# A transformer layer in one core: the sample's gate/up stage started with eight PSUM banks and DVE-made operands, its out operand loaded earlier, GpSimd storing its own sums

## The chip, the core and the metric

The kernel runs on one core of a Trainium2 chip. The core has five engines that work side by side and meet through semaphores: TensorE (PE in the profile) does matmuls into eight PSUM banks; VectorE (DVE) and ScalarE (ACT) do elementwise work and are the two engines here that read PSUM; GpSimd (POOL) does elementwise work between SBUF tiles; SyncE (SP) issues DMAs. ACT and POOL issue DMAs too, each in the order of its own queue. The metric is the device time of one execution in microseconds (us), as a median over executions.

## The reference

One layer of a hybrid encoder, with the same weights for two batches: the prompt ("p", 512 tokens) and the sample ("s", 1024 tokens), width 1024, in float32.

```
h  = rmsnorm(x);  proj = h @ w_in                      # 1024 x 4096
o_hgrn = two-way gated recurrence, 4 heads of 128;  o_na = 2-D neighbourhood attention, 8 heads of 64
x  = x + concat(o_hgrn, o_na) @ w_out                  # 1024 x 1024
h2 = rmsnorm(x)
x  = x + (silu(h2 @ w_gate) * (h2 @ w_up)) @ w_down    # 1024 -> 2816 -> 1024
```

## The kernel before

Every large product keeps float32 accuracy by splitting each operand into a rounded high part (a cast on ACT) and the rest (a subtraction on DVE) and by adding three matmuls: high by high, high by low, low by high. So a tile that a product reads costs one ACT and one DVE instruction first (`split`, `load_w`).

The stages follow each other: input projection with recurrence and attention of the prompt, then of the sample; the prompt's out projection and its 22 gate/up units with the sample's attention woven in; the sample's out projection (`out_units("s", ...)`); its gate/up stage (`gate_s`); the down projection of both (`down_all`). Tile, the layer in which the kernel is written, puts the instructions of each engine in a fixed order by its own estimate of when each can run, and an earlier place in the program gives it precedence. So an engine's order is not the program's, but it can't change at run time. A pool of SBUF tiles that opens where another closed makes its first writers wait for the old tiles' last readers.

The parts that matter here:

- **Out operand of the sample.** `load_oT` reads the attention's result back in 16 pieces of 128x512, by DMAs in POOL's queue into two buffers, and splits each piece on ACT and DVE. The first 8 (tokens 0 to 511) are called for in `late`, four units before the end of the prompt's gate units; the other 8 in `later`, at the start of the out projection. The out projection takes 4 tiles of 128 tokens at a time, each with its own `pd` bank, and DVE's L945 adds the residual and frees the bank.
- **Gate/up of the sample** uses Strassen's scheme in Winograd's form: per pair of output blocks j (11 of them) and per weight w (0 gate, 1 up), seven products P1 to P7 of 12 matmuls each instead of eight. Their token-side operands are A11, A12, A22 and four sums S1 = A21+A22, S2 = S1-A11, S3 = A11-A21, S4 = A12-S2, where A11 to A22 are quarters of the normalized h2 (`araw`, f32). The weight side needs sums too (T2, T3 and two in place), 4 per w. `norm2` normalizes tile t of 128 tokens as the out projection finishes it and lets `gate_s` start at t = 5: A11, A12 (tokens 0 to 511) and the first weights. `run`, called in `tail` after all eight norms, makes A22 and S1 to S4: sums on POOL (L1135, L1137, L1143) and one on DVE (L1136), then splits, and only then goes through the products. P1+P2, P6+P7 and P5+P3 share a bank of each w. Weight sums of all j are POOL's (L1084, L1092), in one buffer `t` for T2 and T3.
- **Stores.** `store_g` makes four sums of each finished block on POOL and stores seven tiles to DRAM, all seven DMAs in ACT's queue (L1027).
- **Down** reads these back (`wst<-g_A`), loads its weights `B`, splits both on ACT and DVE (L1031, L1032), and runs 18 matmuls a step.

## Time and profile before

| | |
|---|---|
| median of 3 runs | 2022.0 us (2020.91 to 2022.23) |
| the profiled execution, its own time | 2023.84 us |
| its span, first to last instruction | 2021.7 us |
| TensorE matmuls busy | 1950.9 us, 96% of the span |
| VectorE, ScalarE, GpSimd busy | 1261.4, 808.1, 384.4 us |
| mean granted TensorE clock | 0.986 of full speed |

The profile holds one execution. A busy TensorE is not TensorE at full speed: the granted clock says whether it ran at 2.4 GHz (1.00) or at 1.2 GHz (0.50). An instruction's row gives its start, its duration, engine, source line, operation and tiles, and in brackets how long its engine had been idle before it and what ended that.

### The profile page before, as it was taken

What the parts mean: (1) busy time and instruction counts of PE and PEld (TensorE: products, weight loads), DVE (VectorE), ACT (ScalarE), POOL (GpSimd) and SP (SyncE); (2) the same over time, 40 slices, a digit from 0 to 9 for tenths busy, and PEclk for the clock granted to TensorE, in tenths of its full rate; (3) what the DMA queues carried; (4) which work ended last, traced back from release to release, by engine and by line L of the source; (5) the groups of instructions that cost most, each with busy time, mean ns of one, the idle gap of its engine ahead of it and who ended that gap; (6) DMA issues with size and microseconds to landing.
All of it is one profiled execution on the core that took longest, in us unless ns stands there. A gap on an engine that the chain in (4) does not pass through costs nothing.

```text
span 2021.7 us, 28466 instructions
## 1 busy us (share of the span) xinstructions
PE 1950.9 (96%) x10546; PEld 1577.8 (78%) x10546; DVE 1261.4 (62%) x2485; ACT 808.1 (40%) x1477; POOL 384.4 (19%) x326
## 2 busy tenths in 40 slices
PE   7999999999999999998999997899999998999998
PEld 5777887778787778777888776678888887888887
DVE  7677535475775757765755238766666664676643
ACT  5544345553443444654554115323233232433332
POOL 1200000000000010010102123454443441642400
PEclk9999999999999999998999999899999999999999
DMA  7832364433123156454555631132332324854443
GB/s 236 267 95 88 95 214 133 128 106 95 32 74 100 32 181 194 128 162 131 155 140 166 217 125 52 42 118 86 118 107 89 110 92 170 270 184 150 138 142 113
DMA packets 235297, 266.54 MB, mean 132 GB/s; under 512 B 19653, under 2 KB 168155, under 8 KB 234903
## 3 DMA queue, kind: packets, MB, share of 16 engines
q1 hardware_dynamic: 188448, 186.30, 30.9%
q10 hardware_dynamic: 41079, 61.27, 8.5%
q0 software_dynamic: 5632, 17.17, 2.6%
q8 instruction: 83, 1.36, 0.3%
q14 instruction: 55, 0.45, 0.1%
HBM read 194.84 MB, written 70.20 MB: 131 GB/s over the span
## 4 chain that ended last, share of the span: by engine, by line
PE 81%; DVE 5%; DMA 5%; issue 4%; ACT 3%; POOL 2%; ACTq 0%; POOLq 0%; DVEq 0%
PE pd L1037 19%; PE pm L1037 13%; PE pd L180 7%; PE pd L181 7%; PE pd L182 7%; PE pd L167 6%; PE pd L168 6%; PE pd L169 6%; PE pm L311 3%; PE pm L599 1%; PE pm L613 1%; PE pm L631 1%; PE pm L446 1%; DMA wst<-in_w_in_dram 1%; DVE w L110 1%
## 5 line engine op out<-in xcount | busy, mean ns | idle before, releaser
L110 DVE TENSOR_TENSOR w<-wst,w 128x1024 fp32r<-128x1024 f32 x128 | 158.6, 1239 | 120.6 <-ACT w L109 113.6
L109 ACT CAST w<-wst 128x1024 fp32r<-128x1024 f32 x128 | 134.2, 1050 | 184.2 <-PE pd L182 71.7
L1037 PE MATMUL pd<-bo,ao 128*128 128x512 f32 x792 | 194.9, 393 | 5.5 <-ACT bo L1031 5.5
L1037 PEld LDWEIGHTS pd<-bo,ao 128*128 128x128 f32 x792 | 150.2, 190 | 37.6 <-ACT bo L1031 5.9
L1037 PE MATMUL pm<-bo,ao 128*128 128x512 f32 x594 | 147.2, 390 | 0.0
L180 PE MATMUL pd<-h2p,w 128*128 128x512 f32 (+1 forms) x368 | 143.3, 389 | 0.6 <-ACT h2p L144 0.5
L181 PE MATMUL pd<-h2p,w 128*128 128x512 f32 (+1 forms) x368 | 141.6, 385 | 0.0
L182 PE MATMUL pd<-h2p,w 128*128 128x512 f32 (+1 forms) x368 | 141.4, 384 | 0.0
L1037 PE MATMUL pd<-opS,w 128*128 128x512 f32 x528 | 132.9, 401 | 7.8 <-DVE u L1154 3.0
L1037 PE MATMUL pm<-opS,w 128*128 128x512 f32 x528 | 129.2, 393 | 2.7 <-DVE opS L1032 1.4
L167 PE MATMUL pd<-w,hs 128*128 128x512 f32 x320 | 131.4, 411 | 0.0
L1037 PEld LDWEIGHTS pm<-bo,ao 128*128 128x128 f32 x594 | 111.8, 188 | 23.3
L1037 PE MATMUL pd<-opA,w 128*128 128x512 f32 x528 | 129.9, 394 | 0.0
L922 POOL DMA_DIRECT2D ost<-ot_p x8 | 4.3, 541 | 647.6 <-ACT Kn L373 632.4
L1037 PEld LDWEIGHTS pd<-opS,w 128*128 128x128 f32 x528 | 101.6, 194 | 32.7 <-DVE opS L1032 4.6
L169 PE MATMUL pd<-w,hs 128*128 128x512 f32 x320 | 126.4, 395 | 0.0
L168 PE MATMUL pd<-w,hs 128*128 128x512 f32 x320 | 126.2, 395 | 0.0
L1037 PEld LDWEIGHTS pm<-opS,w 128*128 128x128 f32 x528 | 99.6, 189 | 25.0 <-DVE opS L1032 2.6
L1037 PEld LDWEIGHTS pd<-opA,w 128*128 128x128 f32 x528 | 99.1, 189 | 24.1 <-ACT s L1181 3.8
L1031 ACT CAST w<-wst 128x512 fp32r<-128x512 f32 x110 | 65.0, 620 | 114.0 <-PE pd L1037 57.6
L1032 DVE TENSOR_TENSOR w<-wst,w 128x512 fp32r<-128x512 f32 x110 | 99.9, 923 | 16.4 <-ACT w L1031 16.0
L1032 DVE TENSOR_TENSOR bo<-B,bo 128x512 fp32r<-128x512 f32 x55 | 50.8, 924 | 76.7 <-ACT bo L1031 76.7
(233 smaller groups left out, 4314.2 us busy)
## 6 DMA issues: line engine op xcount, KB each, us to landing
wst<-in_w_in_dram SPq DMA_DIRECT2D x68, 512.0 KB, 4.1
wst<-in_w_gate_dram SPq DMA_DIRECT2D x44, 512.0 KB, 4.0
wst<-in_w_up_dram SPq DMA_DIRECT2D x44, 512.0 KB, 3.9
wst<-g_S SPq DMA_DIRECT2D x44, 384.0 KB, 3.2
wst<-g_A SPq DMA_DIRECT2D x33, 384.0 KB, 3.8
g_S<-S ACTq DMA_DIRECT2D x44, 256.0 KB, 2.0
pj_s<-ev ACTq DMA_DIRECT2D x40, 256.0 KB, 2.3
bias<-bias_d SPq DMA_DIRECT2D x192, 48.0 KB, 2.6
```

The source lines that it names most:

```text
L109: act.copy(out=w[:, 0, :], in_=s)
L110: dve.tensor_tensor(out=w[:, 1, :], in0=s, in1=f32(w[:, 0, :]), op=ALU.subtract)
L167: pe.matmul(ps, lhsT=xh, rhs=w[:, 0, j, :], start=k == 0, stop=False)
L168: pe.matmul(ps, lhsT=xh, rhs=w[:, 1, j, :], start=False, stop=False)
L169: pe.matmul(ps, lhsT=xl, rhs=w[:, 0, j, :], start=False, stop=k == NK - 1)
L180: pe.matmul(ps[:, ts], lhsT=wv[:, 0, k, :], rhs=xh, start=k == 0, stop=False)
L181: pe.matmul(ps[:, ts], lhsT=wv[:, 0, k, :], rhs=xl, start=False, stop=False)
L182: pe.matmul(ps[:, ts], lhsT=wv[:, 1, k, :], rhs=xh, start=False, stop=k == NK - 1)
L311: pe.matmul(ps[i * 64:i * 64 + 64, c * 64:c * 64 + 64], lhsT=lhsT[:, c * 128 + i * 64:c * 128 + i * 64 + 64], rhs=rhs(c * 128 + i * 64), s ...
L1031: act.copy(out=dst[0], in_=src)
L1032: dve.tensor_tensor(out=dst[1], in0=src, in1=f32(dst[0]), op=ALU.subtract)
L1037: pe.matmul(ps, lhsT=l[a], rhs=r[b_], start=start and i == 0, stop=stop and i == 2, skip_group_check=more)
```

## The change

1. Both halves of the sample's out operand are loaded in `late`, among the prompt's last gate units; the raw quarters of h2 (`araw`) take the place of the second half's pool in `later`.
2. For the first pair (j = 0) the products of both weights alternate: P1, P2, P4 and P5 of gate and up go to eight banks of their own (four `pd`, four `pm`) before any is read; P6, P7 and P3 follow. P1 starts when norm 5 is done; norms 6 and 7 are called for between products.
3. A22 and the sums for S1 to S4 are made on DVE, the first of them in two token parts (0 to 383 of the quarter, then the last 128) in instructions of 2x384, 4x128 or 2x512 columns. S1 and S2 go to the pool of the out operand's second half. The weight sums of j = 0 go to DVE as well; those of j = 1 to 10 stay on POOL.
4. In the later pairs s3 overwrites s1, and there are two buffers for s2.
5. `store_g` leaves the stores of A11 and A22 in ACT's queue and puts the other five (A12, S1 to S4) in POOL's, which made four of them. It serves the prompt's units and the sample's alike.

```
-    xs, h2, gate = {}, {}, {}
+    xs, h2, gate, araw = {}, {}, {}, {}
...
             else:
-                h2[b, u] = [pls["araw"].tile([128, 4, 512], F32, name=f"a{u}{g}")
-                            for g in range(2)]
+                if u == 0:
+                    for k in ((1, 1), (0, 0), (1, 0), (0, 1)):
+                        araw[k] = pls["araw"].tile([128, 4, 512], F32, name="a%d%d" % k)
+                h2[b, u] = [araw[u, g] for g in range(2)]
         sink = to_tiles(h2[b, u], t % 4) if b == "p" else \
...
         for k in ASIDE:
-            act.dma_start(out=g_d[k][j][:, c0:c0 + n], in_={**A, **S}[k])
+            (act if k in ("A11", "A22") else st).dma_start(out=g_d[k][j][:, c0:c0 + n],
+                                                           in_={**A, **S}[k])
...
-        def operand(name, src, where):
+        def place(name, where):
...
                 A[name] = [[t[:, 0, :], t[:, 1, :]] for t in o]
-            elif where == "actR1":
-                o = [pls[where].tile([128, 2, 4, 512], F32R, tag="actT", bufs=2, name=f"op{name}")]
-                A[name] = [[o[0][:, i, k, :] for i in range(2)] for k in range(4)]
             else:
-                o = pls[where].tile([128, 2, 4, 512], F32R, name=f"op{name}")
+                o = pls[where].tile([128, 2, 4, 512], F32R, name=f"op{name}",
+                                    **({} if where == "aop" else {"tag": "actT", "bufs": 2}))
                 A[name] = [[o[:, i, k, :] for i in range(2)] for k in range(4)]
-            for k in range(4):
-                split(A[name][k], src[:, k, :])
+                whole[name] = o
+        whole = {}
+        def fill(name, src, ts=slice(0, 512), step=1):
+            for k in range(0, 4, step):
+                if step == 1:
+                    split([h[:, ts] for h in A[name][k]], src[:, k, ts])
+                else:
+                    ks = slice(k, k + step)
+                    split([whole[name][:, i, ks, ts] for i in range(2)], src[:, ks, ts])
...
-        def weights(wsrc, j):
+        def weights(wsrc, j, eng):
...
             def sub(o, x, y):
-                pool.tensor_tensor(out=o, in0=x, in1=y, op=ALU.subtract)
+                eng.tensor_tensor(out=o, in0=x, in1=y, op=ALU.subtract)
...
                     sub(B["T3"], B["22"], B["12"])
-                    pool.tensor_tensor(out=B["T2"], in0=B["T3"], in1=B["11"], op=ALU.add)
+                    eng.tensor_tensor(out=B["T2"], in0=B["T3"], in1=B["11"], op=ALU.add)
                     sub(B["12"], B["12"], B["11"])
...
                 "P7": "S3"}
-        order = [(0, w, n) for n, w in (("P1", 0), ("P1", 1), ("P2", 0), ("P2", 1))]
-        order += [(0, w, n) for w in range(2) for n in ("P4", "P6", "P5", "P7", "P3")]
+        order = [(0, w, n) for n in ("P1", "P2", "P4", "P5", "P6", "P7", "P3") for w in range(2)]
         order += [(j, w, n) for j in range(1, NP) for w in range(2)
...
                 if (j, w) not in made:
-                    made[j, w] = weights((w_g, w_u)[w], j)
+                    made[j, w] = weights((w_g, w_u)[w], j, pool if j else dve)
                 ready.append(made[j, w](p))
...
+        ps = {}
+        def begin(n, w, f):
+            ps[n, w] = f()
+            product(ps[n, w], n, ready.pop(0), False)
         def start():
-            operand("A11", raw[0, 0], "x1_s")
+            place("A11", "x1_s")
+            fill("A11", raw[0, 0])
             ahead(2)
-            operand("A12", raw[0, 1], "actR1")
+            place("A12", "actR1")
+            fill("A12", raw[0, 1])
             ahead(4)
+            place("A22", "actR1")
+        def sums(ts, step):
+            a11, a21, a22 = raw[0, 0], raw[1, 0], raw[1, 1]
+            for k in range(0, 4, step):
+                ks = slice(k, k + step)
+                dve.tensor_tensor(out=a22[:, ks, ts], in0=a21[:, ks, ts], in1=a22[:, ks, ts],
+                                  op=ALU.add)
+        def sums2(ts, step):
+            a11, a21, a22 = raw[0, 0], raw[1, 0], raw[1, 1]
+            for k in range(0, 4, step):
+                ks = slice(k, k + step)
+                dve.tensor_tensor(out=a21[:, ks, ts], in0=a11[:, ks, ts], in1=a21[:, ks, ts],
+                                  op=ALU.subtract)
+                dve.tensor_tensor(out=a11[:, ks, ts], in0=a22[:, ks, ts], in1=a11[:, ks, ts],
+                                  op=ALU.subtract)
         def run():
+            first, rest = slice(0, 384), slice(384, 512)
             raw.update({(1, g): h2["s", 1][g] for g in range(2)})
-            operand("A22", raw[1, 1], "actR1")
-            for k in range(4):
-                a11, a12, a21, a22 = (raw[i][:, k, :] for i in ((0, 0), (0, 1), (1, 0), (1, 1)))
-                pool.tensor_tensor(out=a22, in0=a21, in1=a22, op=ALU.add)
-                dve.tensor_tensor(out=a21, in0=a11, in1=a21, op=ALU.subtract)
-                pool.tensor_tensor(out=a11, in0=a22, in1=a11, op=ALU.subtract)
-            operand("S2", raw[0, 0], "aop")
-            operand("S1", raw[1, 1], "aop")
-            operand("S3", raw[1, 0], "x1_s")
-            for k in range(4):
-                a11, a12 = (raw[0, i][:, k, :] for i in range(2))
-                pool.tensor_tensor(out=a12, in0=a12, in1=a11, op=ALU.subtract)
-            operand("S4", raw[0, 1], "aop")
+            a11, a12, a21, a22 = (raw[i] for i in ((0, 0), (0, 1), (1, 0), (1, 1)))
+            begin("P1", 0, dense_ps)
+            need(("2", "s", 6))
+            fill("A22", a22, first, 2)
+            begin("P1", 1, dense_ps)
+            sums(first, 2)
+            begin("P2", 0, dense_ps)
+            need(("2", "s", 7))
+            close_pool("xn_s")
+            open_pool("aop", "left")()
+            begin("P2", 1, dense_ps)
+            fill("A22", a22, rest, 4)
+            ahead(4)
+            for w in range(2):
+                begin("P4", w, mix_ps)
+            sums(rest, 4)
+            place("S1", "actR2")
+            fill("S1", a22)
+            ahead(4)
+            for w in range(2):
+                begin("P5", w, mix_ps)
+            sums2(first, 2)
+            sums2(rest, 4)
+            place("S2", "actR2")
+            fill("S2", a11)
+            ahead(4)
+            place("S3", "x1_s")
+            fill("S3", a21)
+            place("S4", "aop")
+            for k in range(0, 4, 2):
+                ks = slice(k, k + 2)
+                dve.tensor_tensor(out=a12[:, ks, :], in0=a12[:, ks, :], in1=a11[:, ks, :],
+                                  op=ALU.subtract)
+            fill("S4", a12, step=2)
             close_pool("araw")
...
                 return ev.tile([128, 512], F32, tag=tag, bufs=n, name=tag)
-            sg, G, ps, s = {}, {}, {}, {}
+            sg, G, s = {}, {}, {}
...
                                          op1=ALU.mult)
+            for w in range(2):
+                s[1, w] = tmp("s1", 2)
+                act.copy(out=s[1, w], in_=ps["P1", w])
+                taken(w, "A11", ps["P2", w], s[1, w])
+            for w in range(2):
+                begin("P6", w, dense_ps)
+                s[2, w] = plus(tmp("u2", 2), ps["P6", w], s[1, w])
+            ahead(4)
+            for w in range(2):
+                product(ps["P6", w], "P7", ready.pop(0), True)
+                s[3, w] = plus(s[1, w], ps["P6", w], s[1, w])
+            ahead(7)
+            for w in range(2):
+                taken(w, "A22", ps["P5", w], s[3, w])
+                taken(w, "A21", ps["P4", w], s[3, w])
+                product(ps["P5", w], "P3", ready.pop(0), True)
+                taken(w, "A12", ps["P5", w], s[2, w])
+            store_g(0, 0, 512, G, ev)
             bank = {"P1": "X", "P2": "X", "P4": "W", "P6": "Y", "P7": "Y", "P5": "Z", "P3": "Z"}
-            for j, w, n in order:
+            for j, w, n in order[14:]:
                 ahead(7)
...
                 elif n == "P6":
-                    s[2, w] = plus(tmp("u2", 1), p, s[1, w])
+                    s[2, w] = plus(tmp("u2", 2), p, s[1, w])
                 elif n == "P7":
-                    s[3, w] = plus(tmp("u3", 1), p, s[1, w])
-                    if j == 0:
-                        taken(w, "A21", ps["W", w], s[3, w])
-                        taken(w, "A22", ps["Z", w], s[3, w])
-                elif n == "P5" and j:
+                    s[3, w] = plus(s[1, w], p, s[1, w])
+                elif n == "P5":
                     taken(w, "A22", p, s[3, w])
-                elif n == "P4" and j:
+                elif n == "P4":
                     taken(w, "A21", p, s[3, w])
...
         close_pool("na_s")
-        for n in ("tp", "actR1", "araw"):
+        for n in ("tp", "actR1", "actR2"):
             open_pool(n)()
-        load_oT("s", [(0, "actR1")], "tp", "wst", 2)
+        load_oT("s", [(0, "actR1"), (1, "actR2")], "tp", "wst", 2)
     def later():
-        open_pool("actR2")()
+        open_pool("araw")()
         open_pool("xn_s")()
-        load_oT("s", [(1, "actR2")], "tp", "wst", 2)
     before(us, -4, late)
...
     def tail(ws):
-        need(*[("2", "s", t) for t in range(8)])
-        close_pool("xn_s")
-        close_pool("actR2")
-        open_pool("aop", "left")()
+        need(("2", "s", 5))
         gate["run"]()
-        for n in ("ev1", "actR1", "tp", "aop", "x1_s"):
+        for n in ("ev1", "actR2", "actR1", "tp", "aop", "x1_s"):
             close_pool(n)
...
         open_pool("ph2", "left")()
```

## Rows read from the trace of the kernel before

**Rows 1.** The page: TensorE's busy time, and its tenths in 40 slices of the span.

```profile
PE 1950.9 (96%) x10546; PEld 1577.8 (78%) x10546; DVE 1261.4 (62%) x2485; ACT 808.1 (40%) x1477; POOL 384.4 (19%) x326
...
PE   7999999999999999998999997899999998999998
```

**Rows 2.** Windows by stage: length, busy us (instructions) by engine, granted clock, DMA share, GB/s.

```profile
1136.00:1158.00 22.00, 21.82 (x97) 17.73 (x95) 4.76 (x6) 3.44 (x5) 5.21 (x7) 1.00 0.78 279
1158.00:1180.00 22.00, 16.08 (x60) 12.78 (x61) 7.68 (x11) 5.31 (x8) 4.03 (x8) 0.84 0.53 168
...
1237.60:1255.00 17.40, 9.80 (x44) 7.77 (x42) 14.65 (x32) 9.07 (x20) 5.90 (x5) 0.80 0.30 91
1255.00:1283.00 28.00, 20.24 (x62) 12.85 (x62) 27.59 (x26) 12.51 (x23) 20.25 (x13) 0.82 0.06 19
1283.00:1303.00 20.00, 17.02 (x76) 13.71 (x74) 14.57 (x19) 7.54 (x13) 10.32 (x7) 0.98 0.20 66
1303.00:1329.00 26.00, 24.65 (x93) 19.45 (x94) 18.04 (x23) 6.20 (x11) 12.19 (x8) 0.88 0.37 122
1329.00:1693.50 364.50, 364.46 (x1596) 298.48 (x1594) 225.10 (x298) 102.24 (x181) 152.43 (x106) 1.00 0.30 97
```

**Rows 3.** Timelines by engine around the sample's out projection (PE, DVE, POOL).

```profile
1157.43 0.39 PE L169 MATMUL pd<-w,os 128*128 128x512 f32 x1
1163.92 0.77 PE L167 MATMUL pd<-w,os 128*128 128x512 f32 x1 [6.10 <-DVE x L945]
...
1169.74 0.39 PE L169 MATMUL pd<-w,os 128*128 128x512 f32 x1
...
1163.09 1.28 DVE L945 TENSOR_TENSOR x<-pd,x 128x512 f32<-128x512 f32 x2
...
1078.07 0.55 POOL L922 DMA_DIRECT2D ost<-ot_s  x1 [8.08 <-PE pm L613]
...
1110.49 0.54 POOL L922 DMA_DIRECT2D ost<-ot_s  x1 [0.42 <-DVE os L924]
```

**Rows 4.** Timelines at the start of the sample's gate stage (DVE, PE).

```profile
1241.44 1.23 DVE L130 SCALAR_TENSOR_TENSOR nsm<-nsm 128x1 f32<-128x1 f32 x1
...
1247.38 1.09 PE L141 MATMUL pm<-ident,xn 128*128 128x128 f32 x4 [5.63 <-DVE xn L134]
...
1259.25 6.81 DVE L1136 TENSOR_TENSOR a<-a,a 128x512 f32<-128x512 f32 x4
...
1265.98 16.22 DVE L1032 TENSOR_TENSOR opS<-a,opS 128x512 fp32r<-128x512 f32 x16
```

**Rows 5.** DVE's timeline: prices with GpSimd idle, and one norm's small instructions.

```profile
1173.31 1.22 DVE L110 TENSOR_TENSOR w<-wst,w 128x1024 fp32r<-128x1024 f32 x1 [3.60 <-ACT w L109]
...
1189.19 1.29 DVE L1032 TENSOR_TENSOR w<-wst,w 128x512 fp32r<-128x512 f32 x2
...
1217.95 0.15 DVE L124 SCALAR_TENSOR_TENSOR nsm<-nsm 128x1 f32<-128x1 f32 x1
...
1220.20 1.42 DVE L134 SCALAR_TENSOR_TENSOR xn<-x,nsm,wrow 128x512 f32<-128x512 f32 x2
```

**Rows 6.** Timelines at the end of the gate stage (SP, ACT, PE).

```profile
1676.85 0.33 SPq L1213 DMA_DIRECT2D B<-in_w_down_dram  x1
...
1698.35 0.62 ACT L1031 CAST bo<-B 128x512 fp32r<-128x512 f32 x1 [20.48 <-POOL S L1025]
...
1690.68 2.88 PE L1037 MATMUL pm<-opS,w 128*128 128x512 f32 x12
1699.02 1.52 PE L1037 MATMUL pd<-bo,ao 128*128 128x512 f32 x2 [5.46 <-ACT bo L1031]
...
1706.22 1.08 PE L1037 MATMUL pd<-bo,ao 128*128 128x512 f32 x4
```

**Rows 7.** DMA issues: tile, queue, count, size of one, median us to landing.

```profile
g_S<-S ACTq DMA_DIRECT2D x44, 256.0 KB, 2.0
...
x_s<-x POOLq DMA_DIRECT2D x16, 256.0 KB, 2.7
```

## Prediction, made before the changed kernel was run

> **What bounds the kernel now.** I read the page first. TensorE is busy for 96% of the span and full in nearly every slice [rows 1], so only two things can shorten the kernel: TensorE's idle time, and the time it runs at half clock. The windows by stage show where these lie. In the long middle of the sample's gate stage TensorE is busy for 364.46 of 364.50 us at a clock of 1.00, so 1596 matmuls there give the undisturbed pace, 0.228 us each; nothing that the change does inside that stretch can gain. The loss sits at three joints, and the waits name a different engine at each.
>
> *Start of the second token group of the out projection* [rows 3]: TensorE stops at 1157.8 and starts again at 1163.92, after a wait of 6.10 for DVE's L945, the residual that frees a bank. L945 itself needs nothing late; it stands in DVE's fixed order behind the splits of the out operand's second half, whose DMAs are late. Then the clock is at half (the matmul that follows takes 0.77 instead of 0.39): the 15 matmuls from 1163.92 to 1169.74 and a last pace of 0.23 take 6.05 us instead of 3.4. Loss 6.1 + 2.6 = 8.7.
>
> *Start of the gate stage* [rows 2]: between 1237.6 and 1329.0, 91.4 us, TensorE does 1848 - 1596 = 252 matmuls of the stage (57.5 us at 0.228) and 16 transposes (2 us, an estimate: four take 1.09 with the wait for the last one's end [rows 4]). Loss 32. By the windows 7.6 + 7.8 + 3.0 + 1.4 = 19.7 of it is idle, the other 12.5 ran at a granted clock of 0.80 to 0.88, a mix of the full and the half level. What is late is DVE [rows 4]. TensorE waits 5.63 for a norm whose 128x1 instructions take 1.23 us instead of 0.15 [rows 4, 5], while POOL does weight sums beside it. Then DVE is busy for 27.59 of 28 us, with POOL busy for 20.25 [rows 2]: four 128x512 sums take 6.81, 1.70 each, and 16 splits 16.22, 1.01 each [rows 4], where two with POOL idle take 1.29, 0.65 each [rows 5].
>
> *Start of down* [rows 6]: the last gate matmul ends at 1693.56, the first of down starts at 1699.02, 5.46 idle, and the first step of 18 takes until 1706.22, 7.2 us instead of 4.1. It waited for ACT's cast of `B`, and ACT had been idle for 20.48: its queue held the stores of the last block's sums, each waiting for POOL, in front of the cast. `B` was asked for at 1676.85. Loss 5.5 + 3.1 = 8.6.
>
> Together 49 us can be gained, and no more except by chance among the prompt's attention.
>
> **Out operand earlier.** The eight pieces of the first half were issued between 1078.07 and 1110.49 [rows 3], so 4.6 us each with two buffers; sixteen end at about 1078 + 16 x 4.6 = 1152, and the second token group needs them from 1157.8 on, k block by k block. The cushion is 6 us. The same splits run on ACT and DVE, now beside matmuls of stages in which DVE is idle for most of the time (busy 4.76 of 22 us in the window after [rows 2]). Gain between 0 (the chain comes past 1163) and 8.7; I take 8, the near end, because the late pieces were late for want of memory, not of speed.
>
> **Gate stage on eight banks.** Eight products without any reading of PSUM are 96 matmuls, 21.9 us, and with the transposes TensorE has work from 1237.6 to about 1261. Before, it had 48 matmuls, 10.9 us, before it needed A22. In that time DVE must do all that P6 waits for. Prices with POOL idle [rows 5]: 0.61 to 0.65 for 128x512 back to back, 1.22 for 128x1024, 0.92 between them for 2x384. The list from 1237: two norms, 8.0 (each from 1217.95 to 1221.6, 3.7, less what overlaps, and a residual of 0.6); A22 in parts 2.4; sums for S1 2.4; S1's low part 2.5; sums for S2 and S3, four of 2x384 and two of 4x128, 4.9; S2's low part 2.5; five of the eight weight sums of j = 0 (the gate's first three need only weights that are there before the out projection ends) 3.1; low parts of seven weight tiles 4.4. That is 30, to 1267; P6 takes S2 block by block and can start some 2 us sooner, at 1265. TensorE idles 4 there. P7 needs S3 (2.5), and its bank needs s2 read; the s2 buffers lie in `ev1`, which opens where `araw` was, so I put S4's sums and low part (4.8) in front of it, and A11's two blocks (2.4), three more weight tiles (1.8) and s2 (0.6): 12 us after S2, at 1279, against the end of both P6 at 1270.5. TensorE idles 8 there. P7 and P3 then find their inputs. So 12 of the 32 remain as idle time. For the clock I take 1 more: matmuls slowed in a stretch that DVE bounds only shorten the next wait. Loss 13, gain 19.
>
> The bounds: if DVE were never in the way the gain is 32; if all eight products ran dry and DVE still met POOL at 1.0 to 1.7 each (j = 1's weight sums stay there), the list of 42 takes some 60, the loss is 25 and the gain 7. I take 19, since POOL has no sums of j = 0 left and the measured price with it idle is 0.65.
>
> **Stores in POOL's queue.** ACT keeps two stores, of A11 and A22; the second is ready when P5 of the last block is done, two products (5.5 us) before the stage ends, so the cast of `B` can stand at 1690 and TensorE go from gate to down without a stop. Gain between 0 (other memory, new wait for `B` or the read-back) and 8.6; I take 7.5. In POOL's queue each store costs 0.55 of issue [rows 3], 2.8 a pair. POOL is busy for 152.43 of 364.5 us [rows 2], 16 of 38.4 a pair, so 19 of 38.4: hidden. S4's buffer is that of an earlier sum and waits for its store to land; by ACT's queue 2.0, by POOL's 2.7 for the same 256 KB [rows 7], 0.7 later, behind slack of 19. With the cover gone it would cost 3.5 a pair. The Trainium skill ("DMA: Bandwidth & Descriptors", Specifications and Issuing engine by pattern) speaks against this edit: a simple load or store is to go through the hardware path, which GpSimd's queue is not, and it puts the first byte at about 0.6 us by the one and 1 us by the other. The trace agrees in direction, 2.0 against 2.7. By the page 0.4 x 5 x 11 = 22 us would be added to POOL's transfers over the stage and nothing to the sum, as nobody waits.
>
> In the prompt's gate units the same edit takes five of seven stores out of ACT's way, among attention that costs TensorE a few stops; the fixed orders are made anew there, so I take 0 with 3 either way. The edits of s3 and s2 cost nothing: same instructions, same bytes, two products' time to spare.
>
> **Sum.** 8 + 19 + 7.5 = 34.5 from the profiled execution's own 2023.84 gives 1989.3. It is 1.8 above the median of 2022.0, so by the median 1987.5; I forecast 1988.
>
> **Rivals.** *The up half waits for `t`.* T2 and T3 of up go into the one buffer that gate's P6 and P7 must have read. P7's weight tile needs a slot that P1 frees at about 1243, and its low part stands late in the program, behind S2. If DVE takes it there, at 1261, four sums and a split of up follow and P4 of up starts at 1265, with the order of both gate and up stretched: loss 24 instead of 13, time 1999. For it: DVE has no room from 1237 on. Against: DVE's order before mixes such splits between a norm's small instructions, which leave gaps.
>
> *DVE keeps up.* Those gaps hold the weight work, S4 does not stand before s2, and 4 of the 32 remain: 2022 - 8.7 - 28 - 8.6 = 1977.
>
> *One joint stays.* The sixteen pieces come past 1163 because POOL's queue now holds waiting stores between them, or down's first loads wait for memory that `ev1` and `actR2` hold: 8 less, 1996.
>
> *Slower: POOL bounds the gate stage.* POOL's stores of A12 and S1 to S4 stand in its queue in front of the next pair's weight sums. Where A12 comes late and S4 waits for a buffer, T2 of the next gate weights is late for P6. Slack is 19 a pair; from a delay past that on each us counts ten times, and 4 us a pair would give 1988 + 40 = 2028. Against: POOL is idle for 212 of the 364.5 us there [rows 2], and TensorE waits for nothing in them.
>
> *Nothing.* The three gains are taken by new stops in the same places, 2020: the same few DVE sums bound it.
>
> **How the numbers follow.** Forecast 0.44 (1982 to 1994), up half late 0.20, DVE keeps up 0.13, one joint stays 0.12, POOL bounds 0.07, nothing 0.04. Leaving out the last two and the edges of the others gives a range of 1975 to 2006. 0.2% is 4 us, about what a measurement of this kernel can tell. Faster 0.89, same 0.04, slower 0.07.
>
> **What would show it.** Right: no idle of 6 before L945's bank, the first cast of `B` before the last gate matmul ends, DVE sums of 0.6 to 0.7 each around 1240 to 1270, idle of TensorE before P6 and P7 rather than before P4. Wrong: P4 of up after P6 of gate, the pieces of the out operand past 1158, a new wait for POOL between 1330 and 1690, or stops in the prompt's units that grow by more than 3.

## The result and the profile after

The changed kernel takes 1985.9 us (median of 4, 1983.64 to 1989.93) where the kernel before, run beside it, takes 2022.1: ratio 0.982, interval 0.980 to 0.984. Run again in a later group it had 0.983 (0.982 to 0.985). The forecast was 1988, the range 1975 to 2006.

The profiled execution has a span of 1984.3 and a time of its own of 1986.19. Beside the page of before [rows 1], TensorE's busy time is 1934.2 instead of 1950.9, with the same 10546 matmuls. Of the slices that were not full in the sample's part, the one at the end of its gate stage is full now; the one at its start, from 1240 to 1290, still shows 7:

```profile
PE 1934.2 (97%) x10546; PEld 1570.9 (79%) x10546; DVE 1274.7 (64%) x2499; ACT 808.7 (41%) x1474; POOL 412.4 (21%) x416
...
PE   7999999999999999999999999799999999999999
```

The span is cut at five places that every trace shows: the first matmul of the sample's out projection, the first of its gate stage, the end of the gate stage's last, and the first of down's third step. Lengths in us, one profiled execution each; the labels are those of the experiments below.

| kernel | to out projection | out projection | gate stage | to down's third step | rest |
|---|---|---|---|---|---|
| before | 1135.90 | 101.73 | 455.93 | 16.75 | 311.4 |
| after | 1131.36 | 92.88 | 436.45 | 13.30 | 310.3 |
| after_again | 1136.81 | 92.88 | 436.62 | 13.28 | 310.3 |
| oT_later | 1130.67 | 92.89 | 436.55 | 13.27 | 310.3 |
| p7_first | 1133.57 | 92.86 | 433.63 | 13.31 | 310.3 |
| p7_s4 | 1131.02 | 92.88 | 432.89 | 13.29 | 310.3 |
| sums_pool | 1129.64 | 92.90 | 444.22 | 14.58 | 310.4 |
| wsum_pool | 1137.41 | 93.23 | 441.64 | 14.35 | 310.4 |
| stores_prompt | 1124.46 | 92.89 | 441.63 | 16.24 | 310.4 |
| stores_all_pool | 1128.90 | 92.94 | 436.51 | 13.28 | 310.6 |
| b_stores | 1126.83 | 103.71 | 451.58 | 14.98 | 310.5 |
| b0_early | 1125.45 | 92.87 | 436.44 | 9.16 | 310.3 |
| best | 1127.68 | 92.88 | 437.55 | 9.17 | 310.2 |
| p7_s4_b0 | 1134.13 | 92.90 | 433.62 | 9.18 | 310.3 |

From before to after 8.9 + 19.5 + 3.5 + 1.1 come from the last four columns and 4.5 from the first, 37.4 in all. The middle columns repeat to 0.2 us between after and after_again. The first does not: ten of these kernels have the same instructions up to there (all but before, oT_later, stores_all_pool and b_stores), and it runs from 1124.5 to 1137.4 among them. The two ends of that range, stores_prompt and wsum_pool, ran on one chip. The 1.1 of the last column lies behind the last matmul: from its start to the end of the span it is 5.66 in before and 4.56 in after.

The windows of after, to be laid beside [rows 2], show the stages: out projection (two windows, no idle), gate stage in three pieces, and the long middle.

```profile
1131.40:1153.00 21.60, 21.60 (x97) 17.90 (x96) 5.10 (x7) 1.77 (x3) 7.65 (x12) 1.00 1.01 386
1153.00:1175.00 22.00, 22.00 (x99) 18.23 (x98) 7.90 (x10) 3.16 (x3) 2.11 (x4) 1.00 0.27 91
1224.20:1240.60 16.40, 16.11 (x79) 12.77 (x77) 15.95 (x35) 10.76 (x21) 0.54 (x1) 1.00 0.19 64
1240.60:1253.00 12.40, 5.06 (x14) 3.63 (x14) 12.40 (x22) 7.17 (x14) 0.00 (x0) 0.72 0.15 44
1253.00:1282.40 29.40, 25.52 (x108) 19.78 (x108) 28.42 (x36) 11.40 (x18) 13.74 (x9) 1.00 0.27 89
1282.40:1660.70 378.30, 378.30 (x1670) 313.18 (x1669) 251.90 (x312) 112.60 (x196) 186.75 (x163) 1.00 0.32 105
```

In the changed kernel `split` is L1035 (ACT) and L1036 (DVE), the weight sums are L1096 and L1104, and the matmuls of the products are L1041. TensorE's timeline at the start of the gate stage answers [rows 4]. P1 and P2 of gate and up run nearly through, then P4 of gate; P4 of up waits 7.34 and then runs mostly at half clock, 5.03 instead of 2.88 (in the window from 1240.60 the mean granted clock is 0.72). P5 and P6 follow without a stop, P7 and P3 with four short ones.

```profile
1237.74 2.88 PE L1041 MATMUL pm<-opA,w 128*128 128x512 f32 x12
1247.96 5.03 PE L1041 MATMUL pm<-opA,w 128*128 128x512 f32 x12 [7.34 <-ACT w L1035]
1252.83 5.63 PE L1041 MATMUL pm<-opS,w 128*128 128x512 f32 x24
1258.29 5.60 PE L1041 MATMUL pd<-opS,w 128*128 128x512 f32 x24
1264.81 3.06 PE L1041 MATMUL pd<-opS,w 128*128 128x512 f32 x12 [0.91 <-DVE u L1214]
1268.80 3.01 PE L1041 MATMUL pd<-opS,w 128*128 128x512 f32 x12 [0.93 <-DVE u L1214]
1273.26 3.04 PE L1041 MATMUL pm<-opS,w 128*128 128x512 f32 x12 [1.45 <-DVE sg L1214]
```

DVE's timeline of that stretch says why: it has no gap, and the low part of gate's P7 (the first row), the last to read T3 of gate, stands behind the norms and sums. Only then can T3 and T2 of up be written into the same buffer and P4 of up be split. The prices are those of an idle POOL, 0.62 per 128x512 in the row of four (against 1.01 to 1.70 in [rows 4]). The last row is the second s2 (tile `u`), for which P7 of up waits.

```profile
1242.96 0.68 DVE L1036 TENSOR_TENSOR w<-t,w 128x512 fp32r<-128x512 f32 x1
...
1244.16 0.68 DVE L1096 TENSOR_TENSOR t<-wst 128x512 f32<-128x512 f32 x1
...
1247.78 1.28 DVE L1036 TENSOR_TENSOR w<-wst,w 128x512 fp32r<-128x512 f32 x2
1248.98 2.49 DVE L1036 TENSOR_TENSOR opS<-a,opS 128x512 fp32r<-128x512 f32 x4
...
1251.99 1.89 DVE L1036 TENSOR_TENSOR opS<-a,opS 128x512 fp32r<-128x512 f32 x3
...
1268.06 0.68 DVE L1214 TENSOR_TENSOR u<-pd,s 128x512 f32<-128x512 f32 x1
```

At the start of down (ACT, DVE, PE), against [rows 6], the cast of `B` comes 0.2 after P4 of the last block has ended (1655.09 + 2.72), and DVE's low part is one of its last rows, behind A12 and beside POOL's sums, which stretch it to 1.75. TensorE waits 3.39.

```profile
1650.57 6.50 ACTq L1030 DMA_DIRECT2D g_A<-G  x2
1658.01 0.62 ACT L1035 CAST bo<-B 128x512 fp32r<-128x512 f32 x1 [13.01 <-PE pm L1041]
...
1661.46 1.12 DVE L1229 SCALAR_TENSOR_TENSOR G<-sg,G 128x512 f32<-128x512 f32 x1
1662.51 1.75 DVE L1036 TENSOR_TENSOR bo<-B,bo 128x512 fp32r<-128x512 f32 x1
...
1655.09 2.88 PE L1041 MATMUL pm<-opA,w 128*128 128x512 f32 x12
...
1664.31 4.37 PE L1041 MATMUL pd<-bo,ao 128*128 128x512 f32 x11 [3.39 <-DVE bo L1036]
```

### The profile page after: what moved, and what is told of

It is laid out like the page before. It is cut to its first block, busy times and chain, and to the rows that moved or that the text cites. A ratio compares the mean times of both kernels' runs of the same rounds, so it can differ in the third digit from the quotient of the medians.

```text
span 1984.3 us, 28394 instructions
## 1 busy us (share of the span) xinstructions
PE 1934.2 (97%) x10546; PEld 1570.9 (79%) x10546; DVE 1274.7 (64%) x2499; ACT 808.7 (41%) x1474; POOL 412.4 (21%) x416
## 4 chain that ended last, share of the span: by engine, by line
PE 85%; DVE 7%; DMA 4%; ACT 2%; issue 1%; POOL 0%; ACTq 0%; DVEq 0%; POOLq 0%
PE pd L1041 20%; PE pm L1041 15%; PE pd L180 7%; PE pd L167 7%; PE pd L181 7%; PE pd L182 7%; PE pd L168 6%; PE pd L169 6%; PE pm L311 3%; PE pm L599 1%; PE pm L446 1%; PE pm L613 1%; PE pm L631 1%; DMA wst<-in_w_in_dram 1%; DVE w L110 1%
## 5 line engine op out<-in xcount | busy, mean ns | idle before, releaser
L1041 PE MATMUL pd<-bo,ao 128*128 128x512 f32 x792 | 193.9, 392 | 3.4 <-DVE bo L1036 3.4
L1041 PEld LDWEIGHTS pd<-bo,ao 128*128 128x128 f32 x792 | 149.7, 189 | 35.0 <-DVE bo L1036 3.8
L1041 PE MATMUL pm<-bo,ao 128*128 128x512 f32 x594 | 147.0, 389 | 0.0
L1041 PEld LDWEIGHTS pm<-bo,ao 128*128 128x128 f32 x594 | 111.6, 188 | 23.2
L1041 PE MATMUL pm<-opS,w 128*128 128x512 f32 x528 | 127.0, 390 | 2.0 <-DVE sg L1214 1.4
L1041 PE MATMUL pd<-opS,w 128*128 128x512 f32 x528 | 127.0, 390 | 1.8 <-DVE u L1214 1.8
L1041 PE MATMUL pd<-opA,w 128*128 128x512 f32 x528 | 127.2, 390 | 0.0
L1041 PEld LDWEIGHTS pm<-opS,w 128*128 128x128 f32 x528 | 99.0, 188 | 23.4 <-DVE sg L1214 1.9
L1041 PEld LDWEIGHTS pd<-opS,w 128*128 128x128 f32 x528 | 99.0, 188 | 23.2 <-DVE u L1214 2.7
L1036 DVE TENSOR_TENSOR w<-wst,w 128x512 fp32r<-128x512 f32 x110 | 105.5, 976 | 15.6 <-ACT w L1035 15.2
L1041 PEld LDWEIGHTS pd<-opA,w 128*128 128x128 f32 x528 | 98.9, 188 | 20.4
L1035 ACT CAST w<-wst 128x512 fp32r<-128x512 f32 x110 | 65.0, 619 | 116.9 <-PE pd L1041 55.4
L1036 DVE TENSOR_TENSOR bo<-B,bo 128x512 fp32r<-128x512 f32 x55 | 51.9, 944 | 75.6 <-ACT bo L1035 75.4
```

The costliest lines, as they stand in the source:

```text
L1035: act.copy(out=dst[0], in_=src)
L1036: dve.tensor_tensor(out=dst[1], in0=src, in1=f32(dst[0]), op=ALU.subtract)
L1041: pe.matmul(ps, lhsT=l[a], rhs=r[b_], start=start and i == 0, stop=stop and i == 2, skip_group_check=more)
```

## The experiments

**What holds the start of the gate stage.** In p7_first the first pair's weight tiles are made in another order; the products run in the same one.

```
-        made, ready, todo = {}, [], list(order)
+        todo = [(0, w, n) for n, w in (("P1", 0), ("P1", 1), ("P2", 0), ("P2", 1), ("P4", 0),
+                                       ("P6", 0), ("P7", 0), ("P4", 1), ("P5", 0), ("P5", 1),
+                                       ("P6", 1), ("P7", 1), ("P3", 0), ("P3", 1))] + order[14:]
...
```

> Of the changed kernel, only the order in which the first pair's weight tiles are made changes: P6 and P7 of gate stand ahead of P4 of up, so the buffer of T2 and T3 is read before up needs it. Theory 'order' (the 7.3 us before P4 of up come from P7's low part standing late in DVE's list, and nothing else is late): P4 of up starts without a stop, its half clock goes too, 1986 becomes 1977 (7.3 + 2). Theory 'volume' (DVE is busy without a gap from 1217 to 1268, so the same work put earlier makes the norms, A22, S2 and the u sums later): the stop before P4 shrinks, but stops of about the same sum stand before P2, P4 of gate, P6 or P7: 1984 to 1988.

Ratio 0.982 (0.979 to 0.984), as the changed kernel; by the stage it is 2.8 faster. P4 of up no longer waits; P6 does instead, for ACT's copy that frees P1's bank (TensorE's timeline of p7_first):

```profile
1240.62 5.28 PE L1041 MATMUL pm<-opA,w 128*128 128x512 f32 x22 [0.17 <-DVE opA L1036]
1245.74 5.60 PE L1041 MATMUL pm<-opS,w 128*128 128x512 f32 x24
1258.16 7.75 PE L1041 MATMUL pd<-opS,w 128*128 128x512 f32 x24 [6.82 <-ACT s L1241]
1267.27 5.76 PE L1041 MATMUL pd<-opS,w 128*128 128x512 f32 x24 [1.36 <-DVE u L1221]
```

The theory of the order alone falls: it foretold 9. On ACT that copy stands behind the cast of S4, which waits for S4's sum, last in DVE's list. So p7_s4 also makes that sum ahead of S2's split, and splits S4 before S3.

```
+            for k in range(0, 4, 2):
+                ks = slice(k, k + 2)
+                dve.tensor_tensor(out=a12[:, ks, :], in0=a12[:, ks, :], in1=a11[:, ks, :],
+                                  op=ALU.subtract)
             place("S2", "actR2")
             fill("S2", a11)
             ahead(4)
-            place("S3", "x1_s")
-            fill("S3", a21)
             place("S4", "aop")
-            for k in range(0, 4, 2):
...
             fill("S4", a12, step=2)
+            place("S3", "x1_s")
+            fill("S3", a21)
```

> The kernel p7_first with S4's sum put ahead of the low parts of S2, and S4's split ahead of S3's. Theory 'order on ACT' (the stop of 6.8 before P6 in p7_first comes from the copy of P1 out of its bank, which stands on ACT behind the cast of S4, and that waits for S4's sum at the end of DVE's list): P6 starts at about 1252 instead of 1258, and the gate stage takes 427 instead of 433.6: 6 us under p7_first and 9 under the changed kernel. Rival 'volume': DVE's list up to s2 of up is as long as before, so the stop moves on to P7 or P3, and the gate stage takes 432 to 434.

Ratio 0.981 (0.979 to 0.982); gate stage 432.9, the rival's number. P6 starts 27.6 us after the stage's first matmul (1251.52 - 1223.90) instead of 31.7 in p7_first (1258.16 - 1226.43). So ACT's order held it for 4.1, not for the 6 that the theory gave it, and the time goes to P7 and to half clock (P6's 24 matmuls take 7.34, P7's first 12 take 4.62):

```profile
1251.52 7.34 PE L1041 MATMUL pd<-opS,w 128*128 128x512 f32 x24 [2.69 <-ACT s L1241]
1261.28 4.62 PE L1041 MATMUL pd<-opS,w 128*128 128x512 f32 x12 [2.42 <-DVE u L1221]
1267.54 3.02 PE L1041 MATMUL pd<-opS,w 128*128 128x512 f32 x12 [1.64 <-DVE u L1221]
```

In three orders DVE's last step before P7 of up, the second s2, ends 44.5, 43.2 and 43.6 us after the stage's first matmul (1268.74 - 1224.24 in after, 1269.61 - 1226.43, 1267.48 - 1223.90). Moving work inside the list moves the stop; the end hardly moves. The amount of DVE's work alone does not explain that, though. In p7_s4 the first s2 ends 37.3 after the first matmul (1261.22 - 1223.90) instead of 40.5 in after (1264.75 - 1224.24), and before the second DVE is idle for 3.34, behind a weight tile of the next pair whose T2 POOL makes late.

```profile
1264.56 1.11 DVE L1036 TENSOR_TENSOR w<-t,w 128x512 fp32r<-128x512 f32 x1 [3.34 <-ACT w L1035]
```

**What the move from POOL to DVE is worth.** sums_pool and wsum_pool put parts of it back:

```
-                dve.tensor_tensor(out=a22[:, ks, ts], in0=a21[:, ks, ts], in1=a22[:, ks, ts],
+                pool.tensor_tensor(out=a22[:, ks, ts], in0=a21[:, ks, ts], in1=a22[:, ks, ts],
...
-                dve.tensor_tensor(out=a11[:, ks, ts], in0=a22[:, ks, ts], in1=a11[:, ks, ts],
+                pool.tensor_tensor(out=a11[:, ks, ts], in0=a22[:, ks, ts], in1=a11[:, ks, ts],
...
-                dve.tensor_tensor(out=a12[:, ks, :], in0=a12[:, ks, :], in1=a11[:, ks, :],
+                pool.tensor_tensor(out=a12[:, ks, :], in0=a12[:, ks, :], in1=a11[:, ks, :],
```

> Of the changed kernel, the sums for S1, S2 and S4 go back to POOL (S3's stays on DVE), in the same parts and at the same places. Theory 'contention' (DVE's low price of 0.6 to 0.7 per 128x512 was bought by keeping POOL still): DVE's instructions beside the sums take 1.0 to 1.2 again, POOL's own take 1.3 to 1.7 per 512 columns, S2 is ready some 6 to 10 us later: 1992 to 1998. Rival 'banks alone' (the gain of the gate stage is the eight products without reading PSUM, and the sums may lie anywhere): DVE's list is shorter by 7.2 (2.4 + 2.5 + 2.3), POOL's chain is beside it, and the time is 1981 to 1987.

```
-                    made[j, w] = weights((w_g, w_u)[w], j, pool if j else dve)
+                    made[j, w] = weights((w_g, w_u)[w], j, pool)
```

> Of the changed kernel, the first pair's eight weight sums go back to POOL, all else stays. Contention: 8 x 0.65 = 5 us leave DVE, but they take 1.3 to 1.7 each on POOL, beside the norms' small instructions and A22's parts: the four of gate stretch the start as before the change, the four of up take 6 before P4 of up: 1988 to 1994. Rival 'volume': with 5 us less on DVE the stops before P4 of up, P6 and P7 shrink together: 1981 to 1984.

sums_pool: ratio 0.986 (0.985 to 0.988), gate stage 7.8 longer. wsum_pool: 0.987 (0.985 to 0.989), 5.2 longer. By their times both go the way of contention, though DVE has 7 and 5 us less to do; their traces differ. In sums_pool DVE's instructions grow dearer: nine low parts of 128x512, most of them beside POOL's sums, take 13.59, 1.51 each, where four in after take 2.49. DVE is also idle twice for what POOL's sums hold up, 1.72 and 1.83.

```profile
1253.51 13.59 DVE L1036 TENSOR_TENSOR opS<-a,opS 128x512 fp32r<-128x512 f32 x9 [1.83 <-ACT opS L1035]
...
1252.90 5.16 POOL L1202 TENSOR_TENSOR a<-a,a 128x1024 f32<-128x1024 f32 x2
1258.02 1.71 POOL L1096 TENSOR_TENSOR t<-wst 128x512 f32<-128x512 f32 x1
```

In wsum_pool DVE's instructions up to P4 of up keep their price (three low parts in 1.89), and what it loses there is a wait: the four weight sums of up take 7.1 on POOL (1247.95 to 1255.02), where DVE is through them in 3.1 in after (1244.16 to 1247.25), and DVE is idle for 4.36 until they come. POOL's first sum, beside DVE's low parts, takes 3.29, the other three 1.26 each.

```profile
1247.95 3.29 POOL L1096 TENSOR_TENSOR t<-wst 128x512 f32<-128x512 f32 x1 [14.72 <-ACT opS L1035]
...
1248.23 1.89 DVE L1036 TENSOR_TENSOR opS<-a,opS 128x512 fp32r<-128x512 f32 x3
1254.48 1.91 DVE L1036 TENSOR_TENSOR w<-wst,w 128x512 fp32r<-128x512 f32 x2 [4.36 <-ACT w L1035]
```

The Trainium skill ("SBUF — State Buffer", SBUF: two separate sides) says that a VectorE instruction with two inputs in SBUF and a GpSimd one that reads SBUF use one pair of ports, which the first to start holds to its end. The traces agree that the two slow each other, 1.51 against 0.62 on DVE in sums_pool and 3.29 against 1.26 on POOL in wsum_pool; the lock itself no run here shows.

**What the stores in POOL's queue are worth.** stores_prompt keeps them in the prompt's units only; b_stores puts them, alone, into the kernel before; stores_all_pool moves the last two as well.

```
-            (act if k in ("A11", "A22") else st).dma_start(
+            (act if c0 == 0 or k in ("A11", "A22") else st).dma_start(
```

> Of the changed kernel, the sample's stores all go back to ACT's queue; the prompt's units keep five of seven on POOL. If POOL's stores gave the 3.4 at the start of down: the last block's stores hold ACT's first cast of B again and down starts 3.4 later: 1989. If ACT's casts of down are held by A22's store and the last sums anyway: within 1 of 1986. If POOL's stores in the sample's stage cost anything there: under 1986.

```
-            act.dma_start(out=g_d[k][j][:, c0:c0 + n], in_={**A, **S}[k])
+            (act if k in ("A11", "A22") else st).dma_start(out=g_d[k][j][:, c0:c0 + n],
+                                                           in_={**A, **S}[k])
```

> The kernel before with one part of the change: five of seven stores in POOL's queue. By the stages of stores_prompt against the changed kernel: the two short stops of 0.15 in each of the sample's pairs go (3.2 in all), the start of down takes 9.2 to 9.7 instead of 12.7, the out projection and the start of the gate stage stay as before (101.7, and 32 lost): 5 to 8 us faster than before, ratio 0.996 to 0.9975. Rival: the store queue holds up POOL's sums, which the kernel before needs at the start of the gate stage too: no gain or a loss there.

```
-            (act if k in ("A11", "A22") else st).dma_start(
+            st.dma_start(
```

> The changed kernel with the stores of A11 and A22 in POOL's queue too. Theory 'A22 holds ACT' (ACT's first cast of B came at 1658.0, right after the store of A22 had waited for its block until 1656.7): the cast comes some 6 to 10 us earlier, DVE's low part with it, TensorE goes on without its stop of 3.4, and the start of down takes 5.0 instead of 9.2. Rival 'memory' (the bo tiles lie where the last block's tiles were read): the cast stays within 1 us of the same place and nothing is gained. Between: DVE's low part stays behind A12's last instruction, which ends at 1662.5, and 0 to 1 are gained.

stores_prompt: ratio 0.986 (0.984 to 0.989). Down's third step comes 2.9 later, with the 5.46 of before back at its start. The gate stage is 5.2 longer, which I had not expected: 2.0 in one stop at the second pair, the other 3.2 in the long middle, where TensorE's matmuls show no idle time. The windows of the two kernels show it only in the count, 439 matmuls in 100 us against 443 (stores_prompt, then after):

```profile
1300.00:1400.00 100.00, 99.99 (x439) 81.84 (x438) 62.72 (x83) 28.07 (x50) 46.89 (x34) 1.00 0.34 108
```

```profile
1300.00:1400.00 100.00, 100.00 (x443) 82.84 (x442) 66.53 (x83) 29.35 (x52) 52.64 (x46) 1.00 0.31 101
```

The timelines of stores_prompt around one pair's start (PE, PEld, ACT, POOL) give the mechanism. P2 should follow P6 at 1433.90 (2.72 a product) and starts at 1434.06, because its bank is freed by ACT's copy of P1, and ACT has the last of seven stores in front of the copy, which waits for POOL's fourth sum. The row of the weight loads (PEld) names the wait, 0.43 for that copy.

```profile
1431.18 2.88 PE L1041 MATMUL pd<-opS,w 128*128 128x512 f32 x12
1434.06 3.02 PE L1041 MATMUL pd<-opA,w 128*128 128x512 f32 x12
...
1434.06 2.59 PEld L1041 LDWEIGHTS pd<-opA,w 128*128 128x128 f32 x12 [0.43 <-ACT s L1260]
...
1433.06 0.33 ACTq L1030 DMA_DIRECT2D g_S<-S  x1
1433.42 0.59 ACT L1260 COPY s<-pd 128x512 f32<-128x512 f32 x1 [9.06 <-POOL S L1028]
...
1431.73 1.29 POOL L1028 TENSOR_TENSOR S<-G,S 128x512 f32<-128x512 f32 x1
```

There is one such stop a pair, at P2 of gate: its first matmul starts 0.17 late and its second another 0.11. A pair takes 38.4 us instead of the 38.08 of after, and ten pairs make the 3.2. The kernel before has the same stop and the same 38.4. Its page shows it in the weight loads (the last number is idle time until ACT's copy L1181, nine times 0.4):

```profile
L1037 PEld LDWEIGHTS pd<-opA,w 128*128 128x128 f32 x528 | 99.1, 189 | 24.1 <-ACT s L1181 3.8
```

b_stores: ratio 0.9975 (0.996 to 0.9985), at the edge of what was expected; the gate stage is 4.35 shorter, down's third step comes only 1.8 sooner, and the out projection is 2.0 longer, with 8.1 of waiting for L945, whose cause no run shows. stores_all_pool: 0.982 (0.980 to 0.984) and every stage as in after. ACT's first cast of `B` comes 0.2 us after P4 of the last block ends here too, with no store of A22 in ACT's queue. So A22's store was not the holder; in both traces the wait of that cast is ended by TensorE. By the program's memory map, which no trace shows, the first `bo` tile lies in the last quarter of A22's tile, which P4 reads.

By itself the store is slower in POOL's queue, from issue to landing (the page of after; [rows 7] has 2.0 for ACT's queue):

```profile
g_S<-S POOLq DMA_DIRECT2D x44, 256.0 KB, 2.7
```

**The start of down.** b0_early loads and splits down's first `B` in memory of the gate's weights:

```
                 if n == "P1":
...
+                    if j == NP - 1 and w == 1:
+                        e = pls["tp"].tile([128, 1024], F32, tag="wst", bufs=2,
+                                           name="wst")[:, :512]
+                        ld.dma_start(out=e, in_=w_d[0:128, 0:512])
+                        o = main.tile([128, 2, 1024], F32R, tag="w", bufs=5, name="w")
+                        gate["bo0"] = [o[:, i, :512] for i in range(2)]
+                        split(gate["bo0"], e)
...
+            else:
+                bo = gate["bo0"]
```

> The changed kernel; down's first weight tile B is loaded during the last block, into a buffer of the gate weights, and split there, so that neither its memory (the first bo tile lies where A22 was, which P4 of the last block reads) nor DVE's order holds it. Theory 'memory, then DVE's order' for the 3.4 that are left at the start of down: TensorE goes from the last gate matmul into down's first step without a stop, and the start of down takes 4.1 to 6.5 instead of 9.2 (the second step's tiles still stand behind the last block on DVE, beside POOL). Rival 'DVE beside POOL is the bound there': the stop moves whole to the second step, 8.5 to 9.2 as before.

TensorE goes on without a stop (1651.88 + 2.72) and waits 0.86 at the second step; the third comes 9.16 after the gate stage instead of 13.30. Ratio 0.982 (0.980 to 0.984): a gain of 4 is less than the interval, so it is read from the stage. The edit moves both `B`'s memory and its place in DVE's order; what each is worth alone was not tried.

```profile
1651.88 2.88 PE L1041 MATMUL pm<-opS,w 128*128 128x512 f32 x12
1654.61 2.88 PE L1041 MATMUL pd<-w,ao 128*128 128x512 f32 x12
1657.33 1.52 PE L1041 MATMUL pm<-w,ao 128*128 128x512 f32 x6
1658.68 0.61 PE L1041 MATMUL pd<-bo,ao 128*128 128x512 f32 x2
1660.16 2.56 PE L1041 MATMUL pd<-bo,ao 128*128 128x512 f32 x10 [0.86 <-DVE bo L1036]
```

**The out operand, and the start of the out projection.** oT_later calls for the second half where the kernel before did, but in the memory of the changed one; after_again is the changed kernel once more.

```
-        load_oT("s", [(0, "actR1"), (1, "actR2")], "tp", "wst", 2)
+        load_oT("s", [(0, "actR1")], "tp", "wst", 2)
     def later():
...
         open_pool("xn_s")()
+        load_oT("s", [(1, "actR2")], "tp", "wst", 2)
```

> The changed kernel with the second half of the out operand called for at the start of the out projection again, but into the pool that is now open early. If memory was what made the pieces late (as the prediction had it): Tile can issue them when the buffers are free, and the out projection up to the gate's first matmul takes 92.9 again, within 1. If the place of the call decides: the second token group stops for 4 to 7 us again and it takes 97 to 102.

> The changed kernel itself, beside the others of this group. Both theories: 1986 by its own first runs, 0.982 of the kernel before. The start of its out projection is the question: four kernels that are the same up to there had it at 1124.5 to 1137.4. If that is chance of the single execution, this one lies in the same band; if the 4.5 gained there belong to the change, at 1131 again.

The out projection takes 92.89, to 0.01 as in after: with the memory free the place of the call makes no difference. The last of the 16 pieces is issued at 1126.53 there, 4.1 before the out projection starts; in after it is this row of POOL, 5.2 before (1131.36):

```profile
1126.18 0.54 POOL L922 DMA_DIRECT2D ost<-ot_s  x1 [1.66 <-DVE os L924]
```

The start of after_again's out projection, 1136.81, is even later than that of the kernel before, with the same program as after's 1131.36.

**A better version.** Two attempts. The one called best puts p7_s4 and b0_early together and makes P3's weight tiles sooner (`ahead(6)` instead of `ahead(4)` behind S2's split); p7_s4_b0 leaves that last step out.

> p7_s4 with the weight tiles of P3 made ahead of the splits of S4 and S3, and with b0_early. If the stop before P7 of up (1.6, and the half clock around it) in p7_s4 came from a low part of the next pair's weights that waited for POOL in front of s2 of up: the gate stage takes 428 to 431 instead of 432.9, and with the start of down 7 to 11 us are gained on the changed kernel: ratio 0.977 to 0.979. If DVE's volume sets it: 432 to 433 and 4 to 7 gained.

> p7_s4 and b0_early together, with the weight tiles of P3 back behind the splits (in the kernel called best, ACT took a cast of the next pair's T2, which waited 9.6 for POOL, ahead of the copies that free P6's banks). If the two gains are of different joints: the gate stage takes 432.9 as in p7_s4, and from its end to the third step of down 9.2 instead of 13.3 as in b0_early; 3.6 + 4.1 = 7.7 less than the changed kernel at the same start of the out projection, a ratio of about 0.978. If the earlier work of down changes ACT's or DVE's order in the last pair: the gate stage over 434.

best: 0.982 (0.980 to 0.983); gate stage 437.6, outside both expectations. With P3's tiles made sooner, ACT's order takes a cast of the next pair's T2 ahead of the copies that free P6's banks, and this cast waits 9.62 for POOL; TensorE waits 12.89 (ACT's and PE's timelines of best):

```profile
1257.26 0.62 ACT L1035 CAST w<-t 128x512 fp32r<-128x512 f32 x1 [9.62 <-POOL t L1104]
1257.78 1.06 ACT L1241 COPY s<-pd 128x512 f32<-128x512 f32 x2
...
1258.41 12.73 PE L1041 MATMUL pd<-opS,w 128*128 128x512 f32 x48 [12.89 <-ACT s L1241]
```

p7_s4_b0: 1975.0 (median of 5) where before has 2020.1, ratio 0.978 (0.976 to 0.980), below the intervals of after and after_again. Both gains stand: gate stage 433.6, third step of down after 9.18. It beats both kernels.

## Why the prediction was right, point by point

- **The total** (34.5 forecast, 37.4 between the profiles, 36.2 between the medians) is right, in part by luck. The terms of the out operand and of the stores have the right size, though more than half of what the stores give comes at a place where the prediction had seen nothing. The term of the gate stage is 4 to 5 too large. The difference is filled by small gains that no term held: 0.9 more at the out operand, 1.1 behind the last matmul, and the 3 to 4.5 of the first column, which can't be told from chance.
- **Out operand earlier, 8 of 8.7.** Measured 8.9, with no idle in the two windows. "Late for want of memory, not of speed" is borne out by oT_later. The cushion was larger than worked out: the pieces take 3.5 us each (1073.54 to 1126.18 for sixteen), not 4.6, so the last is issued 5.2 before the out projection starts; the forecast had it 16 after (1152 against 1135.90).
- **Gate stage, 19.** Measured 19.5, but it is 16.3 at the start and 3.2 in the middle, and the middle belongs to the stores, as do 2.0 at the second pair. Between kernels that handle the sample's stores alike, the banks and the sums give 14.3 (before and stores_prompt, 455.93 - 441.63) or 15.1 (b_stores and after, 451.58 - 436.45): the term was 4 to 5 too large. The step that failed is "nothing that the change does inside that stretch can gain": 364.46 of 364.50 busy hid one stop of 0.3 a pair, since a matmul's recorded 0.39 runs on past the next one's start, 0.227 later. The pace of 0.228 was not the undisturbed one; after has 38.08 / 168 = 0.2267. The 12.5 at half clock is a slip for 12.3 (32 - 19.7), without effect on the sum.
- **The list of 30 us on DVE.** The low parts of S2 and S3 are all done 29.6 us after the first gate matmul (1253.88 - 1224.24; the rows do not tell the two apart), the first s2 40.5 after it. Forecast were 29.4 for S2's alone, 2.5 more with S3's, and 41.4. So the list held, and was a little shorter than worked out. The prices with POOL idle held. sums_pool shows that they rest on a still POOL.
- **Where TensorE stands idle.** Forecast 4 before P6 and 8 before P7; measured 7.3 before P4 of up, 1.8 before P7, 2.0 before P3, and 2.2 of half clock after the first. The sign "before P6 and P7 rather than before P4" failed. In all 15.4 lost to 1282.45 (58.2, less 180 matmuls at 0.2267 and 2 for the transposes), where 13 was forecast. The mechanism is that of the rival "the up half waits for `t`", milder: the low part of gate's P7 tile came 18.7 after the first gate matmul, not 23.4 (1261 - 1237.6). p7_first and p7_s4 show that taking away this stop of 9 gains 3 to 4: the second s2, and with it P7 of up, stays where it was.
- **Not seen:** P6 needs P1's bank, and the copy that frees it stands behind S4's cast on ACT. In after it just fits; p7_first uncovers it.
- **Stores in POOL's queue, 7.5 at the start of down.** The term was mis-sized in its place: 3.5 there, of which stores_prompt gives the stores 2.9. The cast of `B` came nearly where it was forecast, 2.7 before the stage's end instead of 3.6. What the term left out is DVE's low part of `B`, which stands behind A12 in DVE's fixed order and beside POOL's sums, and ends 3.6 after the stage's end. The prediction's lower bound named "other memory"; the rival "one joint stays" named memory too, of other pools. b0_early takes away memory and order together and gains 4.1. With the gate stage the stores are worth 8.1 (stores_prompt against after, 5.2 + 2.9) or 6.1 (before against b_stores, 4.35 + 1.8): about the forecast's size, at other places.
- **POOL as the bound** did not come: POOL is busy for 186.75 of 378.3, and TensorE waits for nothing there. The same stores of S take 2.7 to landing by POOL's queue against 2.0 by ACT's [rows 7]. The Trainium skill ("DMA: Bandwidth & Descriptors", Issuing engine by pattern) would send a simple store by the hardware path, as generally the faster; the trace agrees in direction. As the prediction had it, the sum does not feel the 0.7, and the queue that waits costs more.
- **The prompt, 0 with 3 either way.** 4.5 between the two profiles. Ten kernels with the same instructions up to there differ by 13, so this number carries nothing. The medians differ by 36.2, of which the later stages make 32.9; the 3 that are left are no more than the interval of the ratio, 3.3 us either way.
- **Open:** why the 1.1 behind the last matmul went, of which b_stores shows 0.9, was not traced. Whether POOL's late T2 is all that keeps p7_s4 from the 427 that was foretold was not tried by itself.

## What to carry to other kernels

A stage in which TensorE is 100% busy can still gain: compare its matmul count per window, or the length of one period, with another kernel's, and read the waits of the weight loads, since a stop of 0.2 to 0.3 us is no idle time in the matmul rows. Where one engine's list sets a joint, taking away the wait that the profile names moves the stop to the next consumer; add up the list to the last consumer before you price the wait. And mind in whose queue a store waits for its data: in ACT's queue it held up the copy that frees a PSUM bank, in the queue of the engine that makes the data it held up nothing of the gate stage.

## What the runs showed of the hardware

Moving 7 us of sums from DVE to a GpSimd that was idle made the stage 7.8 us longer: beside them nine of DVE's remaining instructions went from 0.62 to 1.51 each, and DVE waited 3.6 for what GpSimd's sums held up. One execution of the same instructions differs from the next by up to 13 us before the out projection, on one chip too, while the stages behind it repeat to 0.2; stage lengths told gains of 3 to 4 apart that five rounds of whole times did not.
